# Making GpSimd's low parts of weights and fetched outputs in two instructions of half the columns

## The chip, the cores and the metric

The kernel runs on one core of one Trainium2 chip. The metric is the device time of one execution in microseconds (us); smaller is better. A core has five engines that work side by side: PE (TensorE, the matrix multiplier; its weight loads have a row of their own, PEld), DVE (VectorE), ACT (ScalarE), POOL (GpSimd) and SP (SyncE, which here only issues DMAs). Each engine runs its own instructions in order and waits for the others by semaphores.

## The reference

Two layers of a diffusion backbone run over 512 latent tokens (x) and 256 context tokens (ctx), 1024 channels wide. Layer 0 mixes tokens by differential attention with 8 heads, layer 1 by neighbourhood attention with 16 heads of 64 channels; each is followed by a dense MLP with 4096 hidden channels. Everything is in fp32, and the output is the latent stream after both layers.

```python
for i in range(DEPTH):                       # DEPTH = 2
    ...
    h_l = modulate(rms_norm(x, norm1_g[i]), mod_l[0], mod_l[1])
    h_c = modulate(rms_norm(ctx, norm1_g[i]), mod_c[0], mod_c[1])
    ...
    x = x + mod_l[2] * y_l
    x = x + mod_l[5] * squared_relu_mlp(modulate(rms_norm(x, norm2_g[i]), mod_l[3], mod_l[4]),
                                        w_mlp1[i], w_mlp2[i])
    if need_ctx:
        ctx = ctx + mod_c[2] * y_c
        ...
def squared_relu_mlp(h, w1, w2):
    return jnp.square(jax.nn.relu(h @ w1)) @ w2
```

## The kernel before, in words

**High and low parts.** PE multiplies in a format called fp32r, to which a copy rounds. To stay close to fp32, the kernel keeps most operands as two fp32r tiles: the high part is the value rounded to fp32r, the low part is the value minus the high part. A product is then three matmuls: high by high, high by low, low by high (PASSES). So each weight that comes from memory is split first. `wsplit` (L141 to L152) does it: ACT copies the raw tile into `w[:, 0]` (L146, the high part), and then POOL, or another engine if one is named, subtracts that from the raw tile into `w[:, 1]` (L147, the low part). `wraw` (L127) starts the DMA that brings a raw tile, `wload` (L133) does both. Raw tiles (R, in the first MLP also N) are few: the DMA of a later weight into the same buffer waits until both parts have been made.

**Stages**, by the profile's microseconds. Up to about 25: setup and the transposed normed input. To about 362: the first head and then the heads of layer 0, weights in tiles of 768 columns (WA, WB), low parts on POOL; POOL also does the rotary products (L475 to L485), the power that stands for an inverse square root (`power`, L298) and copies of key parts (L452). To about 550: output projection of layer 0 (`project`, L729): `fetch` (L738) brings a head's output from memory, `split` (L742) makes its two parts, the low one (L746) on POOL or DVE; `gated` (L755) takes the product from PSUM (L757) and adds the old stream (L758); `step` and `end` do the products (L752). To about 1130: the first MLP (`mlp`, L814), 768 tokens. To about 1440: layer 1's heads, whose weights are split by DVE. To about 1520: its output projection. To 1893: the second MLP, 512 tokens.

**The MLPs.** `up` multiplies with w1 (L844, PSUM tiles PD). The second product is done in blocks after Strassen's scheme, with seven products of half size for eight (`products_a`, `products_b`): DVE forms sums and differences of hidden blocks (L922, L933, L937, L940) and of weight blocks (L920, L932, L936, L943); ACT and DVE split the hidden blocks (`parts`: L861 high, L862 low); ACT and POOL split the weight blocks; PE multiplies (L904, PSUM banks PA and PB in turn); DVE adds each product into its sums in SBUF (L910 to L914). `blend` multiplies the sums by the gate (L968) and adds them to the stream, half on POOL and half on DVE (L969). The last two chunks go through `down` (L980, L985, L986). In the first MLP a bias table is also built, with a POOL addition (L596) that is queued behind POOL's last low part (`behind("POOL")`).

**The order.** Within the attention stages the order of PE, SP and POOL is written by hand (strings of steps such as CYCLE0, END1, under `manual_schedule`; `pinned` calls `keep_in_program_order` for the split). In the MLPs a planner orders the instructions of each engine by modelled durations and inserts the semaphores; it tracks dependencies by the region of a tile that is written and read.

Of the kernel before, what the change touches and what calls it, by code (L numbers as in the profile page):

```python
# [10 lines left out]
F32 = mybir.dt.float32  # L11
# [52 lines left out]
class Block:  # L64
# [76 lines left out]
    def wsplit(self, raw, n, tile=None, eng=None, tag='W', pinned=False):  # L141
        nc = self.nc
        w = tile
        if w is None:
            w = self.sbt(tag, [P, 2, 1024 if tag == 'W' else 768], F32R)
        high = nc.scalar.activation(w[:, 0, :n], raw, AF.Copy)  # L146
        low = (eng or nc.gpsimd).tensor_sub(w[:, 1, :n], raw, w[:, 0, :n].bitcast(F32))  # L147
        if pinned:
            self.tc.keep_in_program_order(high)
            self.tc.keep_in_program_order(low)  # L150
        self.last["POOL" if eng is None else "other"] = low
        return w  # L152

# [575 lines left out]
    def project(self, l, wo, oT, t0, xsrc, tag_o, tag_h, tag_p, out):  # L729

        nc = self.nc
        ntok = T - P * t0
        oHL, raws, w0, x0, acc = {}, {}, [], [], {}
        gate = {}

        def fetch(h):  # L738
            st = raws[h] = self.sbt('ST' if 'ST' in self.room else 'N', [P, ntok])
            nc.sync.dma_start(st, oT[h])  # L740

        def split(h, eng):  # L742
            st = raws.pop(h)
            u = oHL[h] = self.sbt(tag_o[h // 4], [P, 2, ntok], F32R)
            self.tc.keep_in_program_order(nc.scalar.activation(u[:, 0, :], st, AF.Copy))  # L745
            self.tc.keep_in_program_order(eng.tensor_sub(u[:, 1, :], st, u[:, 0, :].bitcast(F32)))  # L746

        def part(ps, w, i, hs, first=True, final=True):
            c = P * (i - t0)
            for h in hs:  # L750
                for p, (x, y) in enumerate(PASSES):
                    nc.tensor.matmul(ps, oHL[h][:, x, c:c + P], w[h // 2][:, y, 512 * (h % 2):512 * (h % 2) + 512],  # L752
                                     start=(first and h == hs[0] and p == 0), stop=(final and h == hs[-1] and p == 2))

        def gated(ps, x, i, n, src):  # L755
            t = self.sbt('T', [P, 512])
            nc.vector.tensor_mul(t, ps, gate[1 if i < 2 else 0][:, 512 * n:512 * n + 512])  # L757
            nc.vector.tensor_add(x, src, t)  # L758

        def weights(k):  # L760
            w0.append(self.wload(wo[0, k], 1024, eng=(nc.vector, nc.gpsimd)[k % 2 if l == 0 else 1]))

        def begin():
            weights(3)
            gate.update(self.load_gates(l, 0, (0, 1) if t0 == 0 else (0,)))

        def step(j):
            i, half = j // 2, j % 2
            if half == 0:
                acc[i] = self.pst('A')  # L770
                part(acc[i], w0, i, range(3), final=False)
                return
            if i == t0:
                x0.extend(self.sbt(tag_h[0], [P, 3, 512], F32) for _ in range((NT - t0 + 2) // 3))
            part(acc[i], w0, i, range(3, 6), first=False)
            x = x0[(i - t0) // 3][:, (i - t0) % 3, :]
            nc.sync.dma_start(x, xsrc(i)[:, 0:512])
            gated(acc.pop(i), x, i, 0, x)

        def split_last(st, j):  # L780
            if KT - 1 not in oHL:
                oHL[KT - 1] = self.sbt(tag_o[1], [P, 2, ntok], F32R)
            u, cc = oHL[KT - 1], slice(256 * j, 256 * j + st.shape[1])
            nc.scalar.activation(u[:, 0, cc], st, AF.Copy)
            nc.vector.tensor_sub(u[:, 1, cc], st, u[:, 0, cc].bitcast(F32))

        def end():
            w1 = [self.wload(wo[1, s], 1024) for s in range(4)]
            nx = 2 * (NT - t0)
            xu = [self.sbt('EX'[j % 2], [P, 3, 512]) for j in range((nx + 2) // 3)]  # L790
            xh = {(i, n): xu[(2 * (i - t0) + n) // 3][:, (2 * (i - t0) + n) % 3, :]
                  for i in range(t0, NT) for n in range(2)}
            for i in range(t0, NT):
                ps = self.pst('A')
                part(ps, w0, i, (6, 7))
                gated(ps, xh[i, 0], i, 0, x0[(i - t0) // 3][:, (i - t0) % 3, :])
            hT = [self.sbt(tag_h[kt // 4], [P, 2, T], F32R) for kt in range(KT)]
            out.extend((xh, hT))
            for i in range(t0, NT):
                nc.sync.dma_start(xh[i, 1], xsrc(i)[:, 512:1024])  # L800
                ps = self.pst('A')
                part(ps, w1, i, range(KT))
                gated(ps, xh[i, 1], i, 1, xh[i, 1])
                if l == 0:
                    for n in range(2):
                        nc.scalar.dma_start(self.x1[i][:, 512 * n:512 * n + 512], xh[i, n])
                if i % 2 == 1:
                    xns = [self.normed([xh[j, 0], xh[j, 1]]) for j in (i - 1, i)]
                    self.modulated(xns, (i - 1, i), l, 1, hT, tag_p)

        return dict(weights=weights, begin=begin, fetch=fetch, split=split, step=step, split_last=split_last, end=end)


# [447 lines left out]
```

## Time and profile before

| | |
|---|---|
| median of 3 runs | 1893.06 us (1890.46 to 1893.23) |
| the profiled execution's own time | 1894.65 us |
| its span | 1892.9 us, 27406 instructions |
| granted TensorE clock, mean | 0.977 |
| DMA | 225.95 MB, mean 119 GB/s |
| POOL's low parts of weights (L147) | 135 + 49 of 128x1024, 16 + 16 + 4 of 128x768 |
| POOL's low parts of fetched outputs (L746) | 5 of 128x768, 4 + 3 of 128x512 |
| DVE's low parts of weights (L147) | 28 of 128x768, 2 of 128x1024 |

The profile is of one execution. An engine's busy time does not count waits for semaphores, but it does count what an instruction stands still after it has begun. Lines of a timeline give start, duration, engine, source line, operation, written and read tiles with their shape, the number of instructions merged, and in brackets how long the engine sat idle before and what ended that. Lines of the waits give who waited for whom, in total, how often, and the longest. PE's ends are modelled.

### The profile page before, as it was taken

Reading aid. Unit: us, or ns where it says so; the run is one execution under the profiler, and the core shown is the slowest. Engines: PE = TensorE matmul, PEld = TensorE weight load, DVE = VectorE, ACT = ScalarE, POOL = GpSimd, SP = SyncE. Lnnn points to the kernel's source line nnn. Section 1 sums busy time; section 2 is a strip of 40 time slices with the busy share of each in tenths; the row PEclk is TensorE's granted clock in tenths of the full one; section 3 lists DMA queues with packets and bytes.
Section 4 is the critical chain, followed back from the end, with each engine's and each line's share of the span. In section 5 each row is a group of like instructions: output and inputs, shape, how many; then the busy total and the mean of one; then the engine's idle time right before and its main releaser. Section 6 shows DMA issues by size and latency. Waiting matters only on the chain.

```text
span 1892.9 us, 27406 instructions
## 1 busy us (share of the span) xinstructions
PE 1749.8 (92%) x10046; PEld 1525.5 (81%) x10046; DVE 1348.5 (71%) x2333; ACT 943.3 (50%) x2002; POOL 948.5 (50%) x730
## 2 busy tenths in 40 slices
PE   6989999996999999999998998999998989999988
PEld 5878888885789788889887887988997777777766
DVE  4588777885675565475576776777777768888885
ACT  4476767774343333333333245777777344544432
POOL 3755566553224554554644433343345446776663
PEclk9999999997999999999999998999999989999999
DMA  8122222224426556655641321122112333334331
GB/s 330 42 84 79 87 87 87 74 70 168 160 101 173 167 163 182 170 163 180 190 163 60 117 95 59 57 87 68 64 64 98 133 106 122 123 129 150 133 123 66
DMA packets 88551, 225.95 MB, mean 119 GB/s; under 512 B 9248, under 2 KB 24544, under 8 KB 82272
## 3 DMA queue, kind: packets, MB, share of 16 engines
q1 hardware_dynamic: 78928, 211.19, 34.4%
q10 hardware_dynamic: 9488, 13.00, 1.9%
q8 instruction: 79, 1.29, 0.3%
q14 instruction: 56, 0.46, 0.1%
HBM read 205.91 MB, written 18.25 MB: 118 GB/s over the span
## 4 chain that ended last, share of the span: by engine, by line
PE 62%; DVE 18%; ACT 7%; issue 6%; POOL 3%; DMA 3%; ACTq 0%; SPq 0%; DVEq 0%; POOLq 0%
PE PD L844 20%; PE PA L410 14%; PE PB L904 5%; PE PA L904 4%; PE PA L752 3%; DVE H L862 3%; PE PS L519 2%; PE PA L980 2%; PE PA L259 2%; POOL W L147 2%; DVE Q L912 2%; PE PS L658 2%; PE PB L554 2%; PE PQ L400 1%; ACT W L146 1%
## 5 line engine op out<-in xcount | busy, mean ns | idle before, releaser
L147 POOL TENSOR_TENSOR W<-R,W 128x1024 fp32r<-128x1024 f32 x135 | 349.6, 2603 | 226.9 <-ACT W L146 225.8
L844 PE MATMUL PD<-Q,W 128*128 128x384 f32 (+2 forms) x1992 | 391.2, 347 | 9.7 <-DVE Q L336 5.0
L844 PEld LDWEIGHTS PD<-Q,W 128*128 128x128 f32 x1992 | 347.0, 189 | 40.6 <-issue 7.8
L146 ACT ACTIVATE W<-R 128x1024 fp32r<-128x1024 f32 (+1 forms) x165 | 167.4, 1020 | 203.8 <-PE PD L844 45.9
L904 PE MATMUL PB<-W,H 128*128 128x512 f32 x738 | 193.7, 397 | 16.4 <-DVE Q L912 7.3
L147 POOL TENSOR_TENSOR W<-N,W 128x1024 fp32r<-128x1024 f32 x49 | 121.2, 2474 | 161.0 <-ACT W L146 156.2
L904 PE MATMUL PA<-W,H 128*128 128x512 f32 x732 | 192.2, 397 | 9.4 <-DVE H L912 4.6
L904 PEld LDWEIGHTS PB<-W,H 128*128 128x128 f32 x738 | 138.3, 190 | 50.9 <-DVE Q L912 9.4
L410 PE MATMUL PA<-W,Q 128*128 128x384 f32 (+1 forms) x1008 | 175.3, 326 | 0.4 <-DVE H L623 0.4
L904 PEld LDWEIGHTS PA<-W,H 128*128 128x128 f32 x732 | 136.9, 190 | 44.7 <-issue 7.4
L410 PEld LDWEIGHTS PA<-W,Q 128*128 128x128 f32 x1008 | 159.5, 192 | 0.7 <-DVE H L623 0.7
L298 POOL TENSOR_TENSOR SQ<-SQ,half 128x4 f32<-128x4 f32 (+1 forms) x96 | 94.5, 986 | 129.7 <-DVE SQ L423 128.6
L146 ACT ACTIVATE W<-N 128x1024 fp32r<-128x1024 f32 x49 | 51.9, 1058 | 145.3 <-PE PA L904 48.9
L862 DVE SCALAR_TENSOR_TENSOR H<-N,H 128x512 fp32r<-128x512 f32 (+1 forms) x57 | 93.4, 1641 | 28.3 <-ACT H L861 27.9
L410 PE MATMUL PA<-WB,H 128*128 128x384 f32 x576 | 110.6, 345 | 0.8 <-DVE Q L471 0.8
L752 PE MATMUL PA<-W,H 128*128 128x512 f32 x384 | 97.1, 402 | 9.0 <-ACT H L745 5.1
L410 PEld LDWEIGHTS PA<-WB,H 128*128 128x128 f32 x576 | 100.8, 192 | 1.8 <-DVE Q L471 1.1
L844 PE MATMUL PD<-H,W 128*128 128x512 f32 (+1 forms) x408 | 94.7, 380 | 0.0
L752 PEld LDWEIGHTS PA<-W,H 128*128 128x128 f32 x384 | 71.4, 191 | 27.3 <-ACT H L745 5.4
L525 ACT ACTIVATE E<-PS,SA 128x768 f32<-128x768 f32 (+1 forms) x96 | 72.8, 758 | 36.3 <-DVE SA L524 33.3
L524 DVE TENSOR_REDUCE SA<-PS 128x1 f32<-128x768 f32 (+1 forms) x96 | 74.5, 776 | 22.6 <-PE PS L519 11.2
L519 PE MATMUL PS<-Q,Q 128*128 128x256 f32 (+1 forms) x320 | 70.5, 353 | 19.3 <-ACT Q L448 10.0
(258 smaller groups left out, 3609.3 us busy)
## 6 DMA issues: line engine op xcount, KB each, us to landing
R<-in_w_dram SPq DMA_DIRECT2D x121, 512.0 KB
M<-in_wmod_dram SPq DMA_DIRECT2D x48, 1024.0 KB
N<-in_w_dram SPq DMA_DIRECT2D x49, 512.0 KB
R<-in_wqa_dram SPq DMA_DIRECT2D x32, 384.0 KB
R<-in_wqb_dram SPq DMA_DIRECT2D x32, 384.0 KB
Y<-in_rpb_dram SPq DMA_DIRECT2D x48, 128.0 KB
bias<-Y SPq DMA_DIRECT2D x48, 128.0 KB
X<-bias SPq DMA_DIRECT2D x8, 768.0 KB
```

What stands on the lines that cost most here:

```text
L146: high = nc.scalar.activation(w[:, 0, :n], raw, AF.Copy)
L147: low = (eng or nc.gpsimd).tensor_sub(w[:, 1, :n], raw, w[:, 0, :n].bitcast(F32))
L259: nc.tensor.matmul(ps[32 * q:32 * q + 32, 0:256], self.silu[:, kt, :], raws[kt], start=kt < 4, stop=kt >= 4)
L298: nc.gpsimd.tensor_tensor(r, ss, self.half[:, :n], op=ALU.pow)
L410: nc.tensor.matmul(acc[:, :n], hT[kt][:, x, P * i:P * i + P], w[kt // 2][:, y, o:o + n], start=(kt == 0 and p == 0), stop=(kt == KT - 1 an ...
L519: nc.tensor.matmul(s[:, c0:c1], q[:, m, P * i:P * i + P], k[:, m, c0:c1], start=p == 0, stop=p == 1)
L524: nc.vector.tensor_reduce(mx, s, op=ALU.max, axis=AX, negate=True)
L525: nc.scalar.activation(e[:, m, :nk], s, AF.Exp, bias=mx[:, 0:1], accum_out=sm[:, m:m + 1])
L752: nc.tensor.matmul(ps, oHL[h][:, x, c:c + P], w[h // 2][:, y, 512 * (h % 2):512 * (h % 2) + 512], start=(first and h == hs[0] and p == 0), ...
L844: nc.tensor.matmul(ps[:, at:at + b1 - b0], w[kt // 4][:, x, o:o + P], hT[kt][:, y, b0:b1], start=(kt == 0 and p == 0), stop=(kt == KT - 1 ...
L862: nc.vector.scalar_tensor_tensor(u[:, 1], src, 1.0, u[:, 0].bitcast(F32), op0=ALU.mult, op1=ALU.subtract)
L904: nc.tensor.matmul(ps, u[:, x, f, P * i:P * i + P], w[:, y, 512 * f:512 * f + 512], start=(f == 0 and p == 0), stop=(f == 1 and p == 2))
```

## The change

Where POOL makes a low part, it does so in two instructions, one for the first half of the columns and one for the second. Low parts that DVE makes stay whole. What is computed does not change.

```diff
         high = nc.scalar.activation(w[:, 0, :n], raw, AF.Copy)
-        low = (eng or nc.gpsimd).tensor_sub(w[:, 1, :n], raw, w[:, 0, :n].bitcast(F32))
+
+        cuts = ((0, n),) if eng is not None and eng is not nc.gpsimd else ((0, n // 2), (n // 2, n))
         if pinned:
             self.tc.keep_in_program_order(high)
-            self.tc.keep_in_program_order(low)
+        for o, e in cuts:
+            low = (eng or nc.gpsimd).tensor_sub(w[:, 1, o:e], raw[:, o:e], w[:, 0, o:e].bitcast(F32))
+            if pinned:
+                self.tc.keep_in_program_order(low)
         self.last["POOL" if eng is None else "other"] = low
         return w
...
             self.tc.keep_in_program_order(nc.scalar.activation(u[:, 0, :], st, AF.Copy))
-            self.tc.keep_in_program_order(eng.tensor_sub(u[:, 1, :], st, u[:, 0, :].bitcast(F32)))
+            cuts = ((0, ntok // 2), (ntok // 2, ntok)) if eng is nc.gpsimd else ((0, ntok),)
+            for o, e in cuts:
+                self.tc.keep_in_program_order(eng.tensor_sub(u[:, 1, o:e], st[:, o:e], u[:, 0, o:e].bitcast(F32)))
```

## The prediction

> **What bounds the kernel now.** I read the page first, then the busy time by stage, then who PE waits for in each stage, then the timelines of PE, DVE and POOL around those waits. The page's busy row:
>
> ```profile
> PE 1749.8 (92%) x10046; PEld 1525.5 (81%) x10046; DVE 1348.5 (71%) x2333; ACT 943.3 (50%) x2002; POOL 948.5 (50%) x730
> ```
>
> TensorE is busy 92% of the span, so a change on POOL can only win where PE stands still for it. By stage (columns: PE, PEld, DVE, ACT, POOL busy, then clock), the two MLPs:
>
> ```profile
> 546.00:1062.00 516.00, 498.53 (x2815) 430.98 (x2814) 319.61 (x404) 180.52 (x232) 259.30 (x134) 0.99 0.53 161
> ...
> 1525.00:1860.00 335.00, 317.95 (x1393) 256.88 (x1392) 283.67 (x285) 148.14 (x202) 213.03 (x82) 0.98 0.36 121
> ```
>
> PE stands still for 17.5 us of the first MLP and 17 us of the second. DVE is busy 62% there and 85% here. Who PE waits for, in the first and then in the second MLP (us in total, times, longest):
>
> ```profile
> PE PA L904 <- DVE H L912: 4.6, 3, 2.4
> PE PB L904 <- DVE H L912: 3.9, 4, 2.4
> PE PB L904 <- DVE E L912: 3.4, 1, 3.4
> PE PS L330 <- DVE N L313: 2.1, 2, 1.4
> PE PB L904 <- DVE H L862: 1.8, 1, 1.8
> ```
> ```profile
> PE PB L904 <- DVE Q L912: 7.3, 4, 3.6
> PE PA L904 <- DVE Q L912: 3.0, 4, 0.9
> PE PD L844 <- ACT W L146: 3.0, 3, 1.1
> ```
>
> It waits for DVE, mostly for L912, which empties a PSUM bank. None of the long rows names POOL. So the question is why DVE is late. Two low parts of weights on POOL, and DVE from the second one on (start, us):
>
> ```profile
> 1552.06 2.40 POOL L147 TENSOR_TENSOR W<-R,W 128x1024 fp32r<-128x1024 f32 x1 [0.78 <-ACT W L146]
> 1556.71 2.41 POOL L147 TENSOR_TENSOR W<-R,W 128x1024 fp32r<-128x1024 f32 x1 [2.24 <-ACT W L146]
> ```
> ```profile
> 1556.74 2.92 DVE L862 SCALAR_TENSOR_TENSOR H<-N,H 128x512 fp32r<-128x512 f32 x1
> 1559.59 1.27 DVE L910 COPY Q<-PA 128x512 f32<-128x512 f32 x2
> 1560.79 0.67 DVE L862 SCALAR_TENSOR_TENSOR H<-N,H 128x512 fp32r<-128x512 f32 x1
> ```
>
> The same L862 takes 0.67 us when POOL is idle and 2.92 us when it begins 0.03 us after a low part. That low part ends at 1559.12, and L862 ends 0.54 us later, at 1559.66. So a DVE operation with two inputs in SBUF stands still until the POOL instruction in flight has ended, and then does its own work. The copies from PSUM (L910) are not held. The group of the second MLP shows the size:
>
> ```profile
> L862 DVE SCALAR_TENSOR_TENSOR H<-N,H 128x512 fp32r<-128x512 f32 x52 | 85.5, 1646 | 10.3 <-ACT H L861 9.9
> ```
>
> 52 of them lose 52 x (1.646 - 0.67) = 51 us of DVE. What that does to PE, on DVE and then on PE:
>
> ```profile
> 1566.06 2.90 DVE L862 SCALAR_TENSOR_TENSOR H<-N,H 128x512 fp32r<-128x512 f32 x1
> 1568.88 3.42 DVE L943 TENSOR_TENSOR R<-R,R 128x1024 f32<-128x1024 f32 x1
> ...
> 1574.62 2.84 DVE L862 SCALAR_TENSOR_TENSOR H<-N,H 128x512 fp32r<-128x512 f32 x1
> ```
> ```profile
> 1573.05 1.63 PE L904 MATMUL PA<-W,H 128*128 128x512 f32 x6 [0.71 <-DVE Q L912]
> ...
> 1578.71 1.67 PE L904 MATMUL PB<-W,H 128*128 128x512 f32 x6 [1.30 <-DVE Q L912]
> ```
>
> Two held operations in a row, then PE waits 0.71 us for the evictions queued behind them; one more held operation, then 1.30 us.
>
> **The change part by part.** Every low part that POOL makes becomes two instructions: 135 + 49 weights of 1024 columns, 36 of 768, and 12 fetched outputs, so 232 instructions more. DVE's low parts stay whole. The price of a half comes from these groups:
>
> ```profile
> L147 POOL TENSOR_TENSOR WB<-R,WB 128x768 fp32r<-128x768 f32 x16 | 29.5, 1846 | 5.6 <-ACT WB L146 5.6
> ...
> L746 POOL TENSOR_TENSOR H<-ST,H 128x512 fp32r<-128x512 f32 x4 | 5.2, 1288 | 0.0
> ```
>
> 512 columns take 1.29 us, so a whole of 1024 becomes 2.58 instead of 2.41: +0.17 us. The slope is (1.846 - 1.288) / 256 = 2.18 ns a column, so 384 columns take about 1.01 us and a 768 becomes 2.02 instead of 1.85, +0.17; the fetched outputs of 512 the same. 232 x 0.17 = 39 us more of POOL, 52% busy instead of 50%. I put that at nothing on the path: POOL is idle half of the span, which is the cover. Queued behind each second half on POOL are the next low part, the powers of L298, the rotary products of L481 to L485 and the bias additions of L596; they come 0.17 us later. Without the cover all 39 us would count. No wait is added on any engine. The DMA that refills a raw buffer waits for the second half instead of the whole.
>
> A matmul that reads only the first columns of a low part could start 1.1 us earlier, one that reads the last 0.2 us later. The one place where PE visibly waits for this is the last down product:
>
> ```profile
> 1864.99 6.44 PE L980 MATMUL PA<-W,H 128*128 128x512 f32 x20 [2.60 <-POOL W L147]
> ```
>
> Between -1.1 and +0.8 (three pairs at +0.17, and a DVE operation let in between); I take nothing.
>
> What is won: a held DVE operation now waits for the rest of a half, at most 1.29 us instead of 2.41, so an operation that comes right behind the start of a low part saves 2.41 - 1.29 = 1.1 us. That it gets in at the seam between two POOL instructions which stand back to back is shown here, on POOL, DVE and PE:
>
> ```profile
> 1512.74 7.48 POOL L147 TENSOR_TENSOR W<-R,W 128x1024 fp32r<-128x1024 f32 x3
> ```
> ```profile
> 1512.92 5.10 DVE L313 TENSOR_SCALAR N<-X,SA 128x512 f32<-128x512 f32 x2
> 1517.94 2.42 DVE L335 CAST Q<-Y 128x256 fp32r<-128x256 f32 x1
> ```
> ```profile
> 1520.75 1.01 PE L844 MATMUL PD<-Q,W 128*128 128x256 f32 x3 [4.65 <-DVE Q L336]
> ```
>
> Three low parts in a row, and DVE gets exactly one operation done at each seam. Against this stands a rule of the Trainium skill, GPSIMD Engine Reference, section 2.1 Instruction dispatch: consecutive Pool instructions are no barrier, each of the eight cores goes on to the next as soon as its own share is done. Read strictly, there would be no moment at a seam at which all cores are off SBUF, DVE would wait for the pair, and the sum would be that of the third rival below; the seams at 1512 to 1520 do not agree with that.
>
> The sum, by places:
> - Second MLP: eight waits for L912, 10.3 us. Seven of them come to 10.3 - 3.6 = 6.7, below 1.1 each on average: they close. The longest loses 1.1. Together 7.8, say 8.
> - First MLP: nine waits for L912 and L862, 13.7 us. If each loses at most 1.1: of the 4.6, 1.1 + 2.2; of the 3.9, 1.1 + 1.5; of the 3.4 and the 1.8, 1.1 each; 8.1. DVE is much less busy there and I don't see a held operation ahead of each, so three quarters: 6.
> - Start of the second MLP, the seams above: three held operations in a row, then PE waits 4.65. 3 x 1.1 = 3.3.
> - Output projection of the first layer:
>
> ```profile
> 457.54 2.42 DVE L563 SCALAR_TENSOR_TENSOR O<-O,SO,one 128x128 f32<-128x128 f32 x1 [0.81 <-POOL SO L298]
> ```
> ```profile
> 507.06 2.82 DVE L758 TENSOR_TENSOR X<-Q,T 128x512 f32<-128x512 f32 x1
> ```
> ```profile
> PE PA L752 <- ACT H L745: 5.1, 1, 5.1
> PE PA L752 <- DVE T L757: 3.2, 2, 1.7
> ```
>
> Two held operations, each right ahead of one of these waits: 2 x 1.1 = 2.2.
>
> 8 + 6 + 3.3 + 2.2 = 19.5 us. Next in line are PE's 3.0 us on ACT's high parts, and POOL's own products, which come later. I take 4.5 off for what these give back, bounds 0 and 12: **15 us less**. The profiled execution took 1894.65 us (span 1892.9 and 1.75 around it), 1.6 more than the median 1893.06. 1894.65 - 15 = 1879.65 for such an execution; 1878 for a median.
>
> **The rivals.** First, no change: the waits are only passed on. DVE gets in earlier, but meets the second half with its next operation, and PE, 97% and 95% busy in the MLPs, finds another wait. For it: L943 at 1568.88 was held right after L862 was. Against it: an operation is held by one instruction at most, and the number of DVE operations doesn't grow. 1893 (1889.3 to 1896.8).
>
> Second, slower: the second half starves.
>
> ```profile
> 1854.47 4.09 POOL L969 TENSOR_TENSOR X<-X,Q 128x512 f32<-128x512 f32 x1 [7.25 <-DVE Q L968]
> ```
> ```profile
> DVE N L932 <- DMA N<-in_w_dram: 42.3, 7, 9.8
> ```
>
> Here POOL itself took 4.09 us for 512 columns, because a run of DVE operations kept it out: 4.09 - 1.29 = 2.8 us. With a seam in every low part DVE's run gets in there, the low part ends later, the raw buffer is refilled later, and L932, which already waits 6.0 us for its buffer in each of seven rounds, starts later. At 1.2 us a round in 14 rounds of the two MLPs that is 17 us; if half of it reaches PE, 8 to 9 us, no gain left: 1901. It decides from the point where the later refill makes PE wait for W (ACT L146 or POOL L147) in the MLPs, now 3.0 us on ACT. Against it: 42.3 us of such waiting show up in no long wait of PE.
>
> Third, the change doesn't do what it says: the port isn't free at the seam, and a held operation waits 2.58 instead of 2.41. With the 22 held operations of the sum (8, 9, 3 and 2), 22 x 0.17 = 3.7 us, just at the edge of what can be told: 1897. The seams at 1512 speak against it.
>
> A planner orders the MLPs' instructions, and the halves may shift its order; that has both signs and I give it 6 us each way in the range.
>
> **How the numbers follow.** Forecast 0.69, no change 0.16, starving 0.11, no seam 0.04. About 0.2% (3.8 us) is what a measurement of this kernel can tell from no change: faster 0.69, same 0.16, slower 0.15. The forecast's own range: without the amount given back 19.5 us and with 12 given back 7.5, and 6 for the planner: on the better side 1893 - 25.5 = 1867, on the other 1893 - 7.5 + 6 = 1892, of which the part above 1889 counts with no change; 1867 to 1889. For 8 in 10 I reach below to 1864, since held operations outside the four places are not in the sum, and above to 1895, into the case of no change.
>
> **What would show it.** Right: L147 on POOL as 128x512, twice as often, mean 1.3 to 1.6 us; L862 in the second MLP at a mean near 1.15 instead of 1.65 with its longest near 2.0; DVE's busy time in the second MLP down by 30 us or more at the same count; PE's waits for L912 there under 4 us; the wait of 4.65 at the start of the second MLP near 1.3. Wrong: L862 as long as before (no seam); L862 shorter but PE's idle time the same with other releasers (passed on); L147 halves of 2 us and more and PE waiting for W (starving); or a matmul order in the MLPs that differs from before with new waits (planner).

## The result, and the profile after

The changed kernel takes 1875.86 us (median of 4 runs, 1871.82 to 1880.68), the one before 1892.18 beside it (4 runs, 1890.46 to 1893.23). The ratio is 0.9916 with a 95% interval of 0.9896 to 0.9936, so 16.3 us less. The profiled execution took 1877.93 us with a span of 1876.1. In the changed kernel the line numbers behind L146 are 4 to 6 higher: L147 is L152, L313 is L317, L335 and L336 are L339 and L340, L862 is L868, L912 is L918, L943 is L949, L980 is L986. Its busy row:

```profile
PE 1750.8 (93%) x10046; PEld 1530.5 (82%) x10046; DVE 1265.9 (67%) x2333; ACT 948.6 (51%) x2002; POOL 1025.6 (55%) x962
```

DVE does the same 2333 instructions in 82.6 us less; POOL is busy for 77.1 us more with its 232 extra ones. The two MLPs by stage, with the columns as before:

```profile
546.00:1049.00 503.00, 494.83 (x2810) 429.65 (x2809) 295.14 (x400) 179.52 (x231) 286.97 (x213) 1.00 0.55 164
1520.00:1846.00 326.00, 315.63 (x1380) 256.85 (x1379) 237.59 (x279) 149.09 (x199) 245.43 (x160) 0.98 0.38 123
```

PE stands still for 8.2 us of the first MLP (17.5 before) and for 10.4 of the second (17 before). PE's total busy time is the same (1750.8 us, 1749.8 before); what went is its waiting. Who PE still waits for, in the first and then in the second MLP:

```profile
PE PA L910 <- DVE H L918: 4.0, 3, 2.6
PE PB L910 <- ACT W L146: 1.2, 1, 1.2
...
PE PB L910 <- DVE H L918: 0.6, 1, 0.6
...
PE PB L910 <- DVE H L868: 0.2, 1, 0.2
```
```profile
PE PD L850 <- ACT W L146: 4.9, 6, 1.9
PE PB L910 <- DVE Q L918: 4.4, 2, 2.7
PE PA L910 <- DVE H L868: 1.1, 2, 0.6
```

The waits for DVE's evictions (L918) are down from 11.9 to 4.6 us in the first and from 10.3 to 4.4 in the second. In the second MLP the waits for ACT's high parts rose from 3.0 to 4.9. The groups behind that, from 1513 to 1846 on DVE, and POOL's low parts on the page:

```profile
L868 DVE SCALAR_TENSOR_TENSOR H<-N,H 128x512 fp32r<-128x512 f32 x52 | 59.3, 1146 | 23.2 <-ACT H L867 22.9
...
L949 DVE TENSOR_TENSOR R<-R,R 128x1024 f32<-128x1024 f32 x7 | 16.2, 2309 | 7.1 <-POOL W L152 7.1
```
```profile
L152 POOL TENSOR_TENSOR W<-R,W 128x512 fp32r<-128x512 f32 x270 | 406.6, 1533 | 164.9 <-ACT W L146 162.8
...
L152 POOL TENSOR_TENSOR W<-N,W 128x512 fp32r<-128x512 f32 x98 | 137.8, 1427 | 141.9 <-ACT W L146 141.6
```

L868's mean falls from 1646 to 1146 ns at the same count. A half takes 1533 or 1427 ns on average and not 1288. One pair, on POOL and on DVE, shows both sides:

```profile
1547.32 3.00 POOL L152 TENSOR_TENSOR W<-R,W 128x512 fp32r<-128x512 f32 x2 [1.31 <-ACT W L146]
```
```profile
1547.68 1.49 DVE L868 SCALAR_TENSOR_TENSOR H<-N,H 128x512 fp32r<-128x512 f32 x1
```

L868 begins 0.36 us after the pair and ends at 1549.17, while the pair runs on to 1550.32. DVE was held to the seam only. The pair took 3.00 us where two free halves take 2.58, so POOL stood still for 0.42 us while DVE went through.

The start of the second MLP came out otherwise than forecast. POOL, DVE and PE there:

```profile
1503.15 8.22 POOL L152 TENSOR_TENSOR W<-R,W 128x512 fp32r<-128x512 f32 x6
```
```profile
1503.36 1.52 DVE L317 TENSOR_SCALAR N<-X,SA 128x512 f32<-128x512 f32 x1
1504.79 1.37 DVE L339 CAST Q<-Y 128x256 fp32r<-128x256 f32 x1
1506.08 1.49 DVE L317 TENSOR_SCALAR N<-X,SA 128x512 f32<-128x512 f32 x1
1507.49 1.48 DVE L340 TENSOR_TENSOR Q<-Y,Q 128x256 fp32r<-128x256 f32 x1
1508.89 1.37 DVE L339 CAST Q<-Y 128x256 fp32r<-128x256 f32 x1
1510.18 1.48 DVE L340 TENSOR_TENSOR Q<-Y,Q 128x256 fp32r<-128x256 f32 x1
```
```profile
1509.02 0.68 PE L850 MATMUL PD<-Q,W 128*128 128x256 f32 x3 [3.58 <-DVE Q L340]
1511.71 1.01 PE L850 MATMUL PD<-Q,W 128*128 128x256 f32 x3 [2.01 <-DVE Q L340]
```

There are six halves in a row, and behind each seam exactly one held DVE operation of 1.37 to 1.52 us, where there were three of about 2.5. The row of DVE operations is unbroken and each of them is held, so the next one meets the next half. They pay POOL's whole backlog of 8.22 us, however it is cut, and PE waits 3.58 + 2.01 us instead of 4.65. All of PE's waits from 1500 to 1545 come to 7.6 us, 7.9 before. The rows also show that not only operations with two SBUF inputs are held: the cast L339 reads one tile and takes 0.28 us when POOL is idle (at 1511.58), 1.37 here, and 2.42 beside a whole low part.

The last down product waits less for its low part, 0.94 instead of 2.60:

```profile
1852.12 1.98 PE L986 MATMUL PA<-W,H 128*128 128x512 f32 x6 [0.94 <-POOL W L152]
```

### The profile page after: what moved, and what is told of

The parts are those of the page before. It is cut to its first block, busy times and chain, and to the rows that moved or that the text cites. A ratio compares the mean times of both kernels' runs of the same rounds, so it can differ in the third digit from the quotient of the medians.

```text
span 1876.1 us, 27723 instructions
## 1 busy us (share of the span) xinstructions
PE 1750.8 (93%) x10046; PEld 1530.5 (82%) x10046; DVE 1265.9 (67%) x2333; ACT 948.6 (51%) x2002; POOL 1025.6 (55%) x962
## 3 DMA queue, kind: packets, MB, share of 16 engines
q8 instruction: 79, 1.29, 0.3%
## 4 chain that ended last, share of the span: by engine, by line
PE 62%; DVE 11%; ACT 8%; POOL 8%; issue 6%; DMA 5%; ACTq 0%; POOLq 0%; DVEq 0%
PE PD L850 18%; PE PA L414 14%; POOL W L152 6%; PE PB L910 5%; PE PA L910 5%; PE PA L758 4%; DMA R<-in_w_dram 3%; PE PA L986 2%; PE PB L558 2%; PE PA L263 2%; ACT W L146 2%; PE PS L523 2%; PE PQ L404 1%; PE PS L662 1%; PE PB L707 1%
## 5 line engine op out<-in xcount | busy, mean ns | idle before, releaser
L152 POOL TENSOR_TENSOR W<-R,W 128x512 fp32r<-128x512 f32 x270 | 406.6, 1533 | 164.9 <-ACT W L146 162.8
L146 ACT ACTIVATE W<-R 128x1024 fp32r<-128x1024 f32 (+1 forms) x165 | 168.2, 1023 | 201.0 <-PE PD L850 35.3
L152 POOL TENSOR_TENSOR W<-N,W 128x512 fp32r<-128x512 f32 x98 | 137.8, 1427 | 141.9 <-ACT W L146 141.6
L910 PE MATMUL PB<-W,H 128*128 128x512 f32 x738 | 191.9, 396 | 6.4 <-DVE Q L918 4.4
L910 PE MATMUL PA<-W,H 128*128 128x512 f32 x732 | 191.1, 397 | 5.1 <-DVE H L918 4.0
L910 PEld LDWEIGHTS PB<-W,H 128*128 128x128 f32 x738 | 139.1, 190 | 38.9 <-DVE Q L918 5.3
L910 PEld LDWEIGHTS PA<-W,H 128*128 128x128 f32 x732 | 137.7, 190 | 38.1 <-DVE H L918 5.7
L146 ACT ACTIVATE W<-N 128x1024 fp32r<-128x1024 f32 x49 | 51.9, 1058 | 149.1 <-PE PA L910 66.4
L868 DVE SCALAR_TENSOR_TENSOR H<-N,H 128x512 fp32r<-128x512 f32 (+1 forms) x57 | 66.3, 1167 | 39.8 <-ACT H L867 39.5
L850 PEld LDWEIGHTS PD<-H,W 128*128 128x128 f32 x408 | 75.0, 192 | 14.9
```

The costliest lines, as they stand in the source:

```text
L152: low = (eng or nc.gpsimd).tensor_sub(w[:, 1, o:e], raw[:, o:e], w[:, 0, o:e].bitcast(F32))
L850: nc.tensor.matmul(ps[:, at:at + b1 - b0], w[kt // 4][:, x, o:o + P], hT[kt][:, y, b0:b1], start=(kt == 0 and p == 0), stop=(kt == KT - 1 ...
L868: nc.vector.scalar_tensor_tensor(u[:, 1], src, 1.0, u[:, 0].bitcast(F32), op0=ALU.mult, op1=ALU.subtract)
L910: nc.tensor.matmul(ps, u[:, x, f, P * i:P * i + P], w[:, y, 512 * f:512 * f + 512], start=(f == 0 and p == 0), stop=(f == 1 and p == 2))
```

## The experiments

The theory of the prediction (theory 1 in the expectations) is the hold: a DVE operation with two SBUF inputs is held by the POOL instruction in flight and gets in at the seam, so the length of POOL's pieces decides. Against it stand the early start (theory 2: the first half is ready earlier, so a matmul that reads only it starts earlier) and the planner (theory 3: with more and dearer instructions to place, it happens on a better order). Diffs are against the changed kernel and show only the expression that differs. Busy times are of one profile each, times are medians, ratios are to the kernel before on the same chip, with 95% intervals.

**A seam at the end.** As many instructions, but the cut is 64 columns before the end.

```diff
-((0, n // 2), (n // 2, n))
+((0, n - 64), (n - 64, n))
```

> The seam is moved to the end: the first instruction takes all columns but the last 64, the second the last 64. As many instructions as in the change. Theory 1: a held operation waits up to 2.27 us (960 columns at 2.18 ns and 0.18) instead of 1.29, so nearly all of the gain is gone: 1887 to 1894, DVE busy above 1320 us. Theory 2: nearly all gone as well. Theory 3 (planner's order or number of instructions): 1872 to 1882.

Measured: 1892.77 us, 1.0019 (1.0006 to 1.0033). POOL is busy for 1025.9 us, as in the changed kernel, DVE for 1320.8. L868 from 1513 to 1855:

```profile
L868 DVE SCALAR_TENSOR_TENSOR H<-N,H 128x512 fp32r<-128x512 f32 x51 | 73.5, 1444 | 18.6 <-ACT H L867 18.3
```

As many instructions and as much POOL time, but longer holds, give nothing. So the gain hangs on where the seam is, as the hold has it, and not on the number of instructions. It is not a pure control: even this seam relieves DVE by 28 us, and the waits of PE for ACT's W in the second MLP rose to 6.9.

**The second half first.** The same pieces in the other order, so that an early start would be lost.

```diff
-((0, n // 2), (n // 2, n))
+((n // 2, n), (0, n // 2))
```

> The change with the two halves in the other order: the second half of the columns first. Same instructions, same durations, same seam; but the matmuls, which begin with the first columns, now have to wait for both. It tells apart what the run with odd and even columns mixed (there a half took 1.53 us instead of 1.29 and nothing could start early). Theory 1 (the seam alone): 1873 to 1880. Theory 2 (the early start on the first half carries the gain, and its absence cost 30 us and more in that run): 1890 or more. Between them, 1881 to 1889: both count.

Measured: 1877.02 us, 0.9912 (0.9893 to 0.993), DVE 1262.1. This is the same as the change, so an early start on the first columns isn't what wins.

The order that the planner chose can be read from the profiles, by comparing the instructions of an engine in order of start. The change does have another order of products than before, at 388 of PE's 10046 places. The reversed halves differ from before at 94 places only, and win as much. Against the cut at the end they differ in 27 of DVE's 2333 operations and at 116 places of PE, and that cut wins nothing. So a better order isn't the cause either.

**Only the 1024-column weights.** Weights of 768 columns and fetched outputs stay whole.

```diff
-        cuts = ((0, n),) if eng is not None and eng is not nc.gpsimd else ((0, n // 2), (n // 2, n))
+        cuts = ((0, n),) if n < 1024 or (eng is not None and eng is not nc.gpsimd) else ((0, n // 2), (n // 2, n))
...
-            cuts = ((0, ntok // 2), (ntok // 2, ntok)) if eng is nc.gpsimd else ((0, ntok),)
+            cuts = ((0, ntok),)
```

> Only the weights of 1024 columns are halved (MLPs and output projections); the weights of 768 in the attention stages and the fetched outputs stay whole. After the change the first attention stage ended 2.3 us later than before and the second one lost 2.5 us. Theory 1a (those losses come from the halves made there): 1870 to 1874. Theory 1b (they are scatter of the executions): 1874 to 1879.

Measured: 1874.22 us, 0.9915 (0.9895 to 0.9935), POOL 1014.3. The 48 other cuts, of the weights of layer 0's heads and of the fetched outputs, give nothing that can be measured.

**One MLP alone.** Halves in the first MLP only, then in the second only; whole everywhere else. A flag that `mlp` sets, here for the first layer, chooses the cuts.

```diff
+        self.halve = l in (0,)
...
-        cuts = ((0, n),) if eng is not None and eng is not nc.gpsimd else ((0, n // 2), (n // 2, n))
+        cuts = ((0, n), ) if not self.halve or (eng is not None and eng is not nc.gpsimd) else ((0, n // 2), (n // 2, n))
```

> Halves only in the first MLP (w1, w2 and their block differences), whole low parts everywhere else. By the change's profile the first MLP was 12.9 us shorter: theory 1 says 1878 to 1882. If the gain of that stage was the planner's luck in one kernel, 1884 or more.

> Halves only in the second MLP. By the change's profile the loop of the second MLP was 5.6 us shorter and its last down product 2.1: 1883 to 1888. With the 8 us of the forecast it would be 1884; if the gains of the two MLPs don't add, 1889 or more.

Measured: 1884.86 us, 0.9955 (0.9938 to 0.9972), and 1887.3 us, 0.9959 (0.9945 to 0.9972), that is 8.5 and 7.8 us of the 1894.36 that the kernel before took on that chip. Together that is 0.86%, and the change's own gain is 0.84%: it lies in the two MLPs and adds up. The first run missed its expectation: 1884.86 falls in the range named for luck. That range was set by the 12.9 us of one profile, and a single profile of this stage is not that exact, as the last run shows.

**Finer cuts.** Quarters of everything; quarters of the 1024-column weights alone; eighths of those.

```diff
-((0, n // 2), (n // 2, n))
+tuple((n // 4 * k, n // 4 * (k + 1)) for k in range(4))
...
+        cuts = ((0, n),) if n < 1024 or (eng is not None and eng is not nc.gpsimd) else tuple((256 * k, 256 * k + 256) for k in range(4))
...
+        cuts = ((0, n),) if n < 1024 or (eng is not None and eng is not nc.gpsimd) else tuple((128 * k, 128 * k + 128) for k in range(8))
```

> Four instructions of a quarter each. Theory 1: the hold falls to at most 0.77 us (128x256 took 0.73 to 0.77), DVE busy near 1225 us, and PE's remaining waits for DVE in the MLPs, some 8 us, halve: 1868 to 1876. Rival (starving): 4 x 0.77 = 3.1 us of POOL instead of 2.6 for a weight, and DVE gets in at three seams, so weights come later; PE's waits for W (ACT or POOL), 4.9 + 1.9 us in the second MLP after the change, grow by 8 or more: 1880 to 1890.

> Quarters for the weights of 1024 columns, whole low parts for those of 768 and for the fetched outputs. Theory 1 with the attention stages indifferent, as the run with only 1024 columns halved showed: as quarters everywhere, 1868 to 1874. If quarters of the attention weights gave part of that run's gain: 1874 to 1878.

> Eighths of 128 columns for the weights of 1024 columns, the rest whole. A piece of 128 columns takes some 0.46 us (2.18 ns a column and 0.18), a weight 3.7 us of POOL instead of 3.0 in quarters, and POOL was busy 89% of the second MLP's loop with quarters. Theory 1 with starving: the hold falls to 0.46 us but POOL becomes the bound there: 1880 to 1900. Theory 1 without it: as quarters or better, 1862 to 1869.

Measured: 1872.42, 1868.43 and 1918.06 us. The first two lie where theory 1 put them; the eighths miss both of their ranges, on the slow side. The mean and the longest are those of the 53 L862/L868 of the second MLP, in us.

| POOL's low parts | L868 mean | longest | DVE busy | POOL busy | ratio |
|---|---|---|---|---|---|
| whole (before) | 1.639 | 2.93 | 1348.5 | 948.5 | 1 |
| n - 64, then 64 | 1.455 | 2.76 | 1320.8 | 1025.9 | 1.0019 (1.0006 to 1.0033) |
| halves (the change) | 1.148 | 1.84 | 1265.9 | 1025.6 | 0.9916 (0.9896 to 0.9936) |
| quarters | 1.033 | 1.32 | 1228.5 | 1125.4 | 0.9894 (0.9874 to 0.9914) |
| quarters, 1024 only | 0.991 | 1.27 | 1235.6 | 1104.7 | 0.9869 (0.9848 to 0.9891) |
| eighths, 1024 only | 0.845 | 1.05 | 1230.4 | 1218.6 | 1.0121 (1.0099 to 1.0143) |

The hold goes on falling, POOL's time goes on rising, and between quarters and eighths the second overtakes the first. With eighths the first MLP is as short as with quarters (525.8 us from its first to its last w1 product, 527.0 with quarters of 1024, 542.6 before) and the second takes 378.5 (347.5 before). PE's waits from 1518 to 1880 with eighths, and a window of each, quarters (of 1024 only) first:

```profile
PE PA L910 <- POOL W L152: 20.9, 27, 2.1
PE PA L910 <- ACT W L146: 4.9, 4, 3.0
PE PD L850 <- POOL W L152: 3.3, 4, 1.2
```
```profile
1520.00:1820.00 300.00, 288.67 (x1231) 233.49 (x1230) 200.56 (x254) 134.43 (x178) 263.26 (x303) 0.98 0.40 128
```
```profile
1560.00:1850.00 290.00, 260.20 (x1058) 197.54 (x1057) 177.74 (x221) 112.47 (x150) 260.89 (x526) 0.98 0.37 119
```

POOL is busy 88% of that stretch with quarters and 90% with eighths, and PE now waits for POOL by name 31 times. This fits the prediction's second rival, at another cut: low parts come so late that PE starves. The planner is mixed in: with eighths PE's order in the second MLP differs from before at 490 of 1854 places, with quarters at 144. Quarters of the 1024-column weights beat the kernel before and the change.

Not all of these differences is waiting. PE is busy for 1743.4 us with quarters of 1024, 1750.8 with halves and 1768.3 with eighths, for the same 10046 products, at a mean granted clock of 0.984, 0.979 and 0.976. So of the 10.6 us between the profiles of halves and quarters, 7.4 are products that took less time, and not waits that went. Before the change PE's busy time was 1749.8 at 0.977, so in these profiles the change's own gain has no such part. Why the clock differs was not looked into.

**Eighths in the first MLP, quarters behind it.** If the first MLP has room for eighths, this would beat quarters.

```diff
+        s = 128 if self.halve else 256
+        cuts = ((0, n),) if n < 1024 or (eng is not None and eng is not nc.gpsimd) else tuple((o, o + s) for o in range(0, n, s))
```

> Eighths for the weights of the first MLP, where POOL had room for them, quarters for the other weights of 1024 columns, the rest whole. With eighths everywhere the first MLP was 525.8 us, with quarters 527.0, and the second MLP was lost with eighths only. If the shorter hold still pays in the first MLP: 1864 to 1868. If quarters have already taken what there is: 1868 to 1872, the same as quarters.

Measured: 1870.55 us, 0.9862 (0.9839 to 0.9885), no different from quarters. Its first MLP takes 529.5 us in the profile, that of the quarters of 1024 527.0: eighths give no more there.

**Dearer halves.** Two ways to have the change's two pieces, each longer. Even and odd columns; and the reversed halves with 112 columns of overlap, 624 each, which computes the middle columns twice.

```diff
-((0, n // 2), (n // 2, n))
+(slice(0, n, 2), slice(1, n, 2))
...
-((0, n // 2), (n // 2, n))
+((n // 2 - 112, n), (0, n // 2 + 112))
```

> Each low part of POOL is made in two instructions as in the change, but one takes the even columns and the other the odd ones. The seam stays in the middle; a matmul needs both, so nothing can start on the first half. Theory 1 (DVE is held by the POOL instruction in flight, and the seam halves the hold): as the change, 1872 to 1882, L868 in the second MLP at a mean of 1.0 to 1.3 us, DVE busy near 1266 us. Theory 2 (matmuls start earlier on the first half): the gain is gone, 1889 to 1897. Theory 3 (the planner's other order, from more instructions): near the change, with DVE's operations as long as before.

> Contiguous halves in the reversed order, each with 112 columns more than half (they overlap in the middle and write the same values there), so that a half takes about as long as one of odd or even columns did: 512 + 112 = 624 columns at 2.18 ns and 0.18 is 1.54 us. Theory 1b (the run with odd and even columns was slow because its weights came 0.5 us later and POOL became the bound in bursts): near that run, 1905 to 1920. Theory 1c (it was slow for something else in that run, its stride or its order): 1878 to 1890, the longer hold of 1.54 instead of 1.29 costing a third of the gain at most.

Measured: 1917.61 us, 1.0151 (1.0125 to 1.0178), and 1937.57 us, 1.0225 (1.0199 to 1.0251), POOL busy for 1123.8 and 1142.8 us. Both lie outside every range that was expected of them, on the slow side. With them 0.9% of gain becomes a loss of 1.5 and 2.3%, and a piece takes about 1.53 us unhindered instead of 1.29. The hold is not what grew: L868 in the second MLP takes 1.213 and 1.047 us on average, and DVE is busy for 1305.3 and 1286.7 us, less than before. POOL's total doesn't explain it either: quarters have 1104.7 and 1125.4, and gain. PE's waits with the longer halves, from 1547 to 1895:

```profile
PE PD L850 <- ACT W L146: 7.1, 3, 2.8
PE PD L850 <- POOL W L152: 6.3, 3, 3.1
PE PA L910 <- POOL W L152: 5.6, 7, 1.6
PE PA L910 <- DVE Q L918: 3.3, 4, 1.1
```

In the second MLP PE waits for W for 19.0 us, against 4.9 after the change. But the first MLP is as long as before or longer too (548.5 us), with only 2.1 us of waits for POOL's W there. The planner also orders PE otherwise than in the reversed halves, at 498 of the 10046 places. And PE's own busy time is 1769.4 us at a clock of 0.972, against 1752.7 at 0.978 in the reversed halves, 16.7 of the 52 us between the two profiles. How much later weights, the other order and the lower clock cost each couldn't be separated; the cause stays open.

**The kernel before, once more**, to see how far two profiles of one program differ by stage.

> The kernel before, unchanged, for a second profile. In its first profile the first MLP took 542.6 us from its first to its last product with w1; in the run with halves in the second MLP alone, whose first MLP is the same program, 534.9. If stage times scatter by that much between executions, this one lies anywhere from 533 to 544; if the first profile was typical, 541 to 544. DVE busy 1340 to 1355 us, L862 in the second MLP at a mean of 1.6 to 1.7 us.

Measured: 1892.75 us in its one run. The first MLP took 539.4 us, 542.6 in the first profile, and began 1.8 us later; the stages behind it are within 0.6 us. The kernel with halves in the second MLP only has whole low parts and the same order up to there, and took 534.9. The w1 products of the first MLP, with the starts of the first and the last: before, after, and that kernel:

```profile
L844 PE MATMUL PD<-Q,W x1584: 274/337/523, 546.6 to 1089.2; 128*128 128x384 f32 x180, 128*128 128x256 f32 x18
```
```profile
L850 PE MATMUL PD<-Q,W x1584: 274/337/449, 546.3 to 1076.0; 128*128 128x384 f32 x180, 128*128 128x256 f32 x18
```
```profile
L852 PE MATMUL PD<-Q,W x1584: 275/337/450, 548.6 to 1083.5; 128*128 128x384 f32 x180, 128*128 128x256 f32 x18
```

The time lies in the wider of the two ranges expected, and DVE's 1339.0 us just below its own. So one stage of one execution is good to some 8 us, half the whole effect. Stage times below are means over several kernels.

## Why the prediction was right, step by step

It said 1878 (1864 to 1895), and 1875.86 came. The cause is the one named: the held operation waits for the seam. In the second MLP L868's mean, forecast near 1.15, is 1.148; its longest, forecast near 2.0, is 1.84; DVE's time fell by 46 us between the windows shown (over 30 forecast). The cut at the end and the reversed halves, with their orders, speak against the other two theories. The planner's sign of being wrong, another order of products with new waits, came true by half: the order did change, but the only releaser that is new in the rows of the MLPs is ACT's W in the first, with 1.2 us. What the Trainium skill says in GPSIMD Engine Reference, section 2.1 Instruction dispatch, that consecutive instructions are no barrier, did not keep DVE out: one DVE operation got in at every seam of the six halves at 1503.

Two readings of the prediction were too narrow. It gave the hold to operations with two SBUF inputs, but the operations of its own seams, L313 and L335, read one tile (L313 one column of another beside it), and they were held. And it took the two copies of L910 as a sign that evictions from PSUM are not held, but POOL was idle while these ran; that evictions are free shows in L912 instead, whose 116 operations in the second MLP took 678 and 676 ns on average before, and 680 and 677 after.

By terms, with the first MLP from its first to its last w1 product: whole 542.6, 539.4 and 534.9, mean 539.0; halves 529.7, 529.0, 530.6 and 531.9, mean 530.3.
- First MLP: 6 forecast; 8.7 by these means, and 8.5 by the kernel that halves there alone. It was sized too small by the "three quarters". The profile with the cut at the end has 534.5, as short as the shortest with whole low parts, so one profile of this stage shows little.
- Second MLP and its start: 8 + 3.3 forecast; from the first to the last w1 product 346.9 on average with whole low parts (347.5, 346.9, 346.2) and 340.9 with halves (342.4, 340.7, 342.4, 337.9), so 6.0. Of the 8, one wait by one, at most 7.4 could go, since two of the seven waits taken as closed were 1.30 and 1.31 us and lose 1.1 at most. The start's 3.3 is the step that failed: the wait was to become 1.3 and is 3.58 + 2.01. There the first rival is right: the hold was passed on, since DVE has one held operation after another. Waits for L918, forecast under 4, are 4.4.
- The last down product, taken at nothing: 26.8 us from the last w1 product to the start of PE's last product with whole low parts, 24.6 with halves, so 2.2 won. Reversed halves win it too, so it isn't an earlier first half; DVE's seams in that stage remain as the cause, which is argued and not shown.
- Output projection of layer 0: 2.2 forecast. PE's two waits there fell from 5.1 + 3.2 to 4.4 + 1.0, one for DVE's H rose by 0.5, so 2.4; but in the second profile of before they are 5.1 + 2.6, and the first MLP starts at 546.3, before at 546.6 and 548.4. So nothing is shown to have been won there.
- POOL: 39 us more forecast, 77.1 measured. A free piece costs what was said; the other 38 us are, by subtraction, POOL standing at the seams while DVE goes through. They cost nothing visible at halves, since POOL has the room.
- Given back: 4.5 forecast. The second MLP with its start and its end was to give 11.3 and gave 8.2; 1.9 of the difference of 3.1 stands as longer waits for ACT's W.

8.7 + 6.0 + 2.2 are 16.9, and 16.3 were measured. That 15 came so close is partly luck: the sum took 2.7 too little in the first MLP, 5.3 too much in the second with its start, 2.2 for a projection where nothing shows, and nothing for the last down product, which won 2.2. Together that is 2.6 too much, and the 4.5 taken off, of which only 1.9 is seen, covered it.

## What to carry to other kernels

Compare the durations of one shape within a profile, alone and beside another engine's instructions. Where the same operation takes 0.67 and 2.92 us, look for the instruction that holds it, and cut that one if its engine has time to spare. Cut until the time stops falling, which here lies between four and eight pieces. Ask of each held operation what stands behind it: a single one gains by the seam, an unbroken row pays the whole backlog. A cut with longer pieces lost all of it and more here, for a reason that stays open.

## What was not expected of the hardware

- Stepping over every second column cost POOL 1.53 us for 512 columns instead of 1.29, 19% more.
- A free piece took 1.29 us with 512 columns, 0.74 with 256 and 0.46 with 128: about 0.18 us each that don't shrink. The means over all pieces from R, with those that stood still for DVE, are 1.53, 0.92 and 0.57.
- The two runs with pieces of 1.53 instead of 1.29 us, two to a low part, have +1.5% and +2.3% in place of -0.9%; the cause is open.
